# Seven weight buffers in place of four in the block-product stage, and token sums issued later in the program

## The chip, the cores and the metric

The kernel runs on one core of one Trainium2 chip. The metric is the device time of one execution in microseconds. A core has five engines with queues of their own, each strictly in order: TensorE (PE in the profile, PEld its weight loads) multiplies, VectorE (DVE) and ScalarE (ACT) work element by element, GpSimd (POOL) does small side work, and SyncE (SP) only issues DMA transfers. Engines wait for each other by semaphores. An instruction whose wait is not over holds back everything behind it in its queue.

## The reference

One layer of an encoder block on 512 tokens of width 1024, in float32: a half-step SwiGLU, a mixing sublayer with two attentions, a second half-step SwiGLU, and a last norm.

```python
h = modulate(rmsnorm(x, ffn1_norm), sh1, sc1)
x = x + 0.5 * g1 * swiglu(h, ffn1_w_in, ffn1_w_out)
h = modulate(rmsnorm(x, mix_norm), sh2, sc2)
...                                   # MLA and chunk attention on h @ w_in, gated and merged
x = x + g2 * (merged @ w_out)
h = modulate(rmsnorm(x, ffn2_norm), sh3, sc3)
x = x + 0.5 * g3 * swiglu(h, ffn2_w_in, ffn2_w_out)     # swiglu: silu(h@w_gate) * (h@w_up), then @ w_out
return rmsnorm(x, final_norm)
```

The change lies around the second SwiGLU: 1024 to 2 x 2816 columns (22 tiles of 128, gate and up), and back to 1024.

## The kernel before

Every float32 operand is cut into a rounded high part and the rest (`split`, L194 to L197: ScalarE casts the high part, VectorE subtracts it for the low part). A product is three matmuls: high by high, high by low, low by high (L212 to L214, and L584 to L586 in the block products). Weights come from HBM by SP into a ring of four buffers of 128x1024 (`raw`, L189 to L192); ScalarE writes `wh` from each and VectorE `wl`, in rings of three.

Around the change the stages follow each other so.

The mixing sublayer's output product (`down` with `w_out`) finishes one tile of 128 tokens after the other. Each is added to x, normed (`norm_token`, L231; the reciprocal root `rstd` is made by GpSimd, L219) and queued for `turn_token` (L244), in which TensorE transposes it, VectorE and ScalarE scale it (L255, L257), and the two split it into `h_hi` and `h_lo`. After tiles 1 and 3, `mix_tokens` (L269) makes sums and differences of the two tiles just done (L275 to L278, on VectorE) and splits four of these into `sum_h` and `sum_l`.

`up_plain` (L540) makes the first two of the 22 column tiles the plain way, in four jobs of 24 matmul pairs or triples each: jobs 0, 1 and 2 first for the first 256 tokens, then for the other 256, and job 3 for all 512 at once. Before jobs 0 and 2 it lets one pending token tile be turned, so that tiles 2 and 3 are transposed between the jobs.

`up_fast` (L570) makes the other 20 column tiles by a two-by-two block scheme with seven products in place of eight (order 1, 5, 6, 3, 7, 2, 4). For each it loads two weight buffers a and b, forms differences of their halves on VectorE (L599, L600, L603), splits a, the differences and b, and runs 84 matmuls of 256 columns. Products 5, 6, 3, 7 use plain tokens or the token sums. ScalarE copies partial results out (L611 to L618) and applies silu (L624, L625).

Then `down` with `w2b` (L637) brings the result back to 1024; its first loads, the gate vector for this sublayer (`ada_acc`, L284, with loads of `w_ada`) and the reload of x (`x_last`, L1068, issued by ScalarE) are mixed into the last block products.

The order on TensorE is that of the code. On VectorE, ScalarE, GpSimd and SP a scheduler sets it when the program is built: it takes work in the order of the code as buffers and data come free by its own estimate. So a line that is moved in the code, or a buffer more, moves other instructions too.

Three buffers matter beside the `raw` ring: two of 128x1024 with the tag `gate` (gate vectors, `vs` of the attention, the last norm's gain `final_gain`), and one with the tag `ada` (`o32` of the attention, then `ada_acc`).

Of the kernel before, what the change touches and what calls it, by code (L numbers as in the profile page):

```python
# [10 lines left out]
F32 = mybir.dt.float32  # L11
# [7 lines left out]
P = 128  # L19
S = 512  # L20
D = 1024
# [129 lines left out]
class Block:  # L151
# [91 lines left out]
    def turn_token(self, t, which, xn):  # L243
        nc = self.nc  # L244
        h32 = xn.rearrange("p (k c) -> p k c", k=KT)
        ts = slice(t * P, (t + 1) * P)
        for g in range(2):
            pt = self.bank("t")
            for j in range(4):
                nc.tensor.transpose(pt[:, j * P:(j + 1) * P], xn[:, (4 * g + j) * P:(4 * g + j + 1) * P], self.ident)  # L250
            for j in range(4):
                k = 4 * g + j
                sc, sh = self.scale[which][:, k:k + 1], self.shift[which][:, k:k + 1]
                if j < TURN_DVE:
                    nc.vector.tensor_scalar(h32[:, k], pt[:, j * P:(j + 1) * P], sc, sh, op0=ALU.mult, op1=ALU.add)  # L255
                else:
                    nc.scalar.activation(h32[:, k], pt[:, j * P:(j + 1) * P], AF.Identity, scale=sc, bias=sh)  # L257
            ks = slice(4 * g, 4 * g + 4)
            self.split(h32[:, ks], self.hH[:, ks, ts], self.hL[:, ks, ts])
        if which == 2:  # L260
            self.mixed.append(h32)
            if t % 2:
                self.mix_tokens(t // 2, *self.mixed[-2:])

    @staticmethod
    def halves(ap):
        return ap.rearrange("p k (a b c) -> p k a b c", a=2, b=2)

    def mix_tokens(self, j, ha, hb):  # L269
        nc = self.nc  # L270
        if not j:
            self.sums = [[self.slot([P, KT // 2, S // 2], F32R, "sum_" + p) for p in "hl"] for _ in range(4)]
        a11, a12, a21, a22 = (h[:, ks] for h in (ha, hb) for ks in (slice(0, 4), slice(4, 8)))
        tt = nc.vector.tensor_tensor
        tt(a22, a21, a22, op=ALU.add)  # L275
        tt(a21, a21, a11, op=ALU.subtract)
        tt(a11, a22, a11, op=ALU.subtract)
        tt(a12, a12, a11, op=ALU.subtract)  # L278
        cs = slice(j * P, (j + 1) * P)
        for (h, l), part in zip(self.sums, (a22, a11, a21, a12)):  # L280
            self.split(part, h[:, :, cs], l[:, :, cs])
# [254 lines left out]
    def up_plain(self, w1, fs, early, flush):  # L536
        nc = self.nc
        jobs = [(f, gu) for f in fs for gu in range(2)]
        ps, units, done = {}, {}, 0

        def mms(job, n0, n1):
            hi, lo = units[job]
            ns = slice(n0, n1)
            for k in range(KT):
                cs = slice(k * P, (k + 1) * P)
                self.mm3(ps[job][:, ns], (hi[:, cs], lo[:, cs]), (self.hH[:, k, ns], self.hL[:, k, ns]),
                         k == 0 and n0 == 0, k == KT - 1 and n1 == S)

        for i, job in enumerate(jobs):
            f, gu = job  # L550
            units[job] = self.unit(D, w1[f, gu])
            ps[job] = self.bank("o" if f % 2 and gu else "mm")
            if i < early:
                if i in flush:
                    self.flush()
                mms(job, 0, S // 2)
                if i < early - 1:
                    continue
                for late in jobs[:early]:
                    mms(late, S // 2, S)  # L560
            else:
                mms(job, 0, S)
            while done < len(fs) and (fs[done], 1) in ps:
                n = fs[done]
                sc = self.sc4((P, S))
                nc.scalar.activation(sc, ps[n, 0], AF.Silu)
                nc.vector.tensor_tensor(self.act_tile(n), sc, ps[n, 1], op=ALU.mult)
                done += 1

    def up_fast(self, w1, fs):  # L570
        nc = self.nc
        work = self.fix.tile([P, 2, 3, 512], F32, tag="x16", name="w_sums")
        hH, hL = (self.halves(z) for z in (self.hH, self.hL))
        plain = lambda k0, b: [[z[:, k0 + k, :, b] for z in (hH, hL)] for k in range(4)]
        mixed = lambda i: [[z[:, k] for z in self.sums[i]] for k in range(4)]
        lefts = {1: plain(0, 0), 2: plain(4, 0), 3: mixed(3), 4: plain(4, 1), 5: mixed(0), 6: mixed(1), 7: mixed(2)}
        left_half = slice(0, 256)

        def product(p, ps, w, start):
            hi, lo = w  # L580
            for k, (lh, ll) in enumerate(lefts[p]):
                cs = slice(k * P, (k + 1) * P)
                mm = nc.tensor.matmul
                mm(ps, hi[:, cs], lh, start=start and k == 0, stop=False, skip_group_check=not start)  # L584
                mm(ps, hi[:, cs], ll, start=False, stop=False, skip_group_check=not start)  # L585
                mm(ps, lo[:, cs], lh, start=False, stop=k == 3, skip_group_check=not start)  # L586

        def parts(src):
            hi = self.ring.tile([P, D], F32R, tag="wh", name="wh")
            lo = self.ring.tile([P, D], F32R, tag="wl", name="wl")  # L590
            self.split(src, hi, lo)
            return [(hi[:, cs], lo[:, cs]) for cs in (slice(0, 512), slice(512, 1024))]

        for n, f in enumerate(fs):
            a, b = (self.raw(D, w1[f, i]) for i in range(2))
            t = work[:, n % 2]
            tt = nc.vector.tensor_tensor
            b21, b12 = b[:, :512], b[:, 512:]
            tt(t[:, 0:2], b12.unsqueeze(1).to_broadcast([P, 2, 512]), a.rearrange("p (i c) -> p i c", i=2), op=ALU.subtract)  # L599
            tt(b12, a[:, 512:], t[:, 0], op=ALU.subtract)  # L600
            w11, w22 = parts(a)
            w1s, w3s = parts(t[:, 0:2].rearrange("p i c -> p (i c)"))
            tt(t[:, 2], b21, b12, op=ALU.subtract)  # L603
            w21, w2s = parts(b)
            last = self.slot([P, 2, 512], F32R, "w_last")
            self.split(t[:, 2], last[:, 0], last[:, 1])
            x, v = self.bank("s")[:, left_half], self.bank("t")[:, left_half]
            z, y = self.bank("mm")[:, left_half], self.bank("o")[:, left_half]
            s = self.sc4((P, 4, 256))
            product(1, x, w11, True)  # L610
            nc.scalar.copy(z, x)  # L611
            product(5, v, w1s, True)
            nc.scalar.copy(s[:, 1], v)
            product(6, x, w2s, False)
            nc.scalar.copy(s[:, 0], x)  # L615
            product(3, v, w22, False)
            product(7, x, w3s, False)
            nc.scalar.copy(y, x)  # L618
            tt(s[:, 2], v, s[:, 0], op=ALU.add)
            product(2, z, w21, False)  # L620
            tt(s[:, 3], x, s[:, 1], op=ALU.add)
            product(4, y, (last[:, 0], last[:, 1]), False)
            g = self.sc4((P, 2, 256))
            nc.scalar.activation(g[:, 0], z, AF.Silu)  # L624
            nc.scalar.activation(g[:, 1], y, AF.Silu)  # L625
            out = self.act_tile(f).rearrange("p (a b c) -> p b a c", a=2, b=2)
            four = lambda q: q.rearrange("p b (a c) -> p b a c", a=2)
            tt(out, four(s[:, 2:4]), four(g), op=ALU.mult)

    def act_parts(self, u):  # L630
        pair = [self.slot([P, 2, S], F32R, "act_" + p) for p in "hl"]
        self.split(self.acts[u], *pair)
        return [[z[:, j] for z in pair] for j in range(2)]

    def down(self, parts, nk, w2, layer, tail, after, lag=0, store=None, side=None):
        nc = self.nc
        nu = nk // 2  # L637
# [399 lines left out]
    def layer(self, banks):  # L1037
        nc, io = self.nc, self.io
# [7 lines left out]
        parts = lambda u: [[acts[2 * u + j][:, i] for i in range(2)] for j in range(2)]  # L1046
        self.down(parts, NF, io["w2a"], 0, 3, lambda t, xn: self.norm_token(t, 1, xn), LAG_DOWN)
        self.mix(lambda t, xn: self.norm_token(t, 2, xn))
        fin = self.fix.tile([P, D], F32, tag="gate", name="final_gain", bufs=2)
        nc.scalar.dma_start(fin, io["final"].to_broadcast([P, D]))  # L1050

        def finish(t, o32):
            z = self.slot([P, D], F32, "out")
# [9 lines left out]
            nc.scalar.dma_start(self.x_home[t], self.x[:, t])  # L1063
        self.up_plain(io["w1b"], range(F2), EARLY_UP, FLUSH_UP)
        self.up_fast(io["w1b"], range(F2, NF))
        self.x = self.fix.tile([P, NT, D], F32, tag="x16", name="x_last")
        for t in range(NT):
            nc.scalar.dma_start(self.x[:, t], self.x_home[t])  # L1068
# [85 lines left out]
```

## Time and profile before

| What | Value |
|---|---|
| Time, median of 3 runs | 1128.69 us (1128.15 to 1130.97) |
| The profiled execution | 1128.05 us, its span 1126.3 us |
| PE busy | 1091.5 us (97%), 5884 matmuls |
| DVE busy | 697.3 us (62%) |
| ACT busy | 525.1 us (47%) |
| POOL busy | 136.9 us (12%) |
| Mean granted TensorE clock | 0.997 of full speed |
| HBM | 142.55 MB read, 132 GB/s over the span |
| Weight load `raw<-w1b` | 512 KB, 3.5 us from issue to landing |

The time is told for the whole execution, the span for the part that the hardware profiler sees; 1.75 us lie around it. The stages named above lie at 756 to 785 us (`up_plain`), 785 to 992 us (`up_fast`) and from 992 us on (`down` with `w2b`). A busy share is an average over stages; where a stage loses time is seen from the stretches in which PE stands still and from what ended each.

### The profile page before, as it was taken

How to read it: one execution, taken by the hardware profiler on the slowest of the kernel's cores; microseconds unless marked ns; L12 is line 12 of the kernel's file. 1: busy time of each engine (PE TensorE's matmuls, PEld its weight loads, DVE VectorE, ACT ScalarE, POOL GpSimd, SP SyncE). 2: the span in 40 equal slices, each digit the busy share in tenths (PEclk: the TensorE clock that was granted, in tenths of full speed). 3: DMA queues.
4: the chain of work that ended last, by engine and by line, in shares of the span. 5: the costliest groups of instructions: out<-in, count | busy, mean ns of one | idle time of the engine just before them, and what ended most of it. 6: DMA issues, size and time to landing. Idle time of an engine off the chain costs nothing.

```text
span 1126.3 us, 15321 instructions
## 1 busy us (share of the span) xinstructions
PE 1091.5 (97%) x5884; PEld 928.9 (82%) x5884; DVE 697.3 (62%) x1170; ACT 525.1 (47%) x963; POOL 136.9 (12%) x126
## 2 busy tenths in 40 slices
PE   5999999999999999999999999999999999999997
PEld 4788888878888898988887888888999999978885
DVE  5886565663232676666677723568777777786724
ACT  5533222223121476666666633346555554654512
POOL 1000000000000012243344354100000000000100
PEclk9999999999999999999999999999999999999999
DMA  9677666663333620112223233522333333484312
GB/s 361 227 255 243 205 206 212 202 222 110 94 94 96 217 94 19 57 57 69 91 77 90 69 103 104 206 87 82 95 112 97 95 111 113 124 268 132 94 56 75
DMA packets 42992, 149.85 MB, mean 133 GB/s; under 512 B 5155, under 2 KB 5155, under 8 KB 42918
## 3 DMA queue, kind: packets, MB, share of 16 engines
q1 hardware_dynamic: 38160, 136.20, 37.6%
q10 hardware_dynamic: 4758, 12.66, 3.1%
q8 instruction: 46, 0.75, 0.3%
q14 instruction: 28, 0.23, 0.1%
HBM read 142.55 MB, written 6.29 MB: 132 GB/s over the span
## 4 chain that ended last, share of the span: by engine, by line
PE 76%; DVE 8%; DMA 8%; ACT 4%; issue 3%; POOL 0%; ACTq 0%; DVEq 0%; POOLq 0%
PE ps_mm L212 11%; PE ps_mm L214 11%; PE ps_mm L213 11%; DMA raw<-w_ada 6%; PE ps_s L213 3%; PE ps_s L214 3%; PE ps_s L212 3%; DVE wl L197 2%; PE ps_s L586 2%; PE ps_t L212 2%; PE ps_t L214 2%; PE ps_t L213 2%; PE ps_s L584 2%; PE ps_s L585 2%; PE ps_o L214 2%
## 5 line engine op out<-in xcount | busy, mean ns | idle before, releaser
L196 ACT CAST wh<-raw 128x1024 fp32r<-128x1024 f32 x170 | 178.1, 1051 | 244.9 <-PE ps_t L214 75.0
L197 DVE TENSOR_TENSOR wl<-raw,wh 128x1024 fp32r<-128x1024 f32 x138 | 168.5, 1224 | 116.8 <-ACT wh L196 116.4
L214 PE MATMUL ps_mm<-h_hi,wl 128*128 128x512 f32 (+1 forms) x464 | 178.9, 386 | 3.0 <-DVE wl L197 2.8
L212 PE MATMUL ps_mm<-h_hi,wh 128*128 128x512 f32 (+1 forms) x464 | 181.3, 391 | 0.0
L213 PE MATMUL ps_mm<-h_lo,wh 128*128 128x512 f32 (+1 forms) x464 | 178.5, 385 | 0.1
L214 PEld LDWEIGHTS ps_mm<-h_hi,wl 128*128 128x128 f32 x464 | 88.0, 190 | 22.6 <-DVE wl L197 3.8
L213 PEld LDWEIGHTS ps_mm<-h_lo,wh 128*128 128x128 f32 x464 | 88.1, 190 | 16.3 <-DVE h_lo L197 0.3
L212 PEld LDWEIGHTS ps_mm<-h_hi,wh 128*128 128x128 f32 x464 | 88.1, 190 | 15.9
L197 POOL TENSOR_TENSOR wl<-raw,wh 128x1024 fp32r<-128x1024 f32 x32 | 77.2, 2414 | 76.7 <-ACT wh L196 73.0
L288 DVE CUSTOM_DVE_ANT_0 raw<-raw,c_row,cols_sb 128x1024 f32<-128x1024 f32 x32 | 41.1, 1285 | 49.9 <-DMA raw<-w_ada 49.9
L219 POOL TENSOR_TENSOR rstd<-ss,neghalf 128x1 f32<-128x1 f32 x16 | 12.1, 758 | 409.9 <-DVE ss L229 400.4
L599 DVE TENSOR_TENSOR w_sums<-raw 128x1024 f32<-128x1024 f32 x20 | 24.5, 1225 | 46.0 <-DMA raw<-w1b 46.0
L196 ACT CAST act<-sc 128x512 fp32r<-128x512 f32 x22 | 13.6, 622 | 81.4 <-DVE sc L504 81.4
L83 ACT ACTIVATE sc<-sc,stat 128x128 f32<-128x128 f32 (+1 forms) x64 | 35.9, 562 | 29.5 <-DVE stat L81 29.3
L586 PE MATMUL ps_s<-sum_h,wl 128*128 128x256 f32 x160 | 44.8, 280 | 1.1 <-DVE wl L197 1.1
L586 PE MATMUL ps_t<-sum_h,wl 128*128 128x256 f32 x160 | 44.9, 281 | 0.4 <-DVE wl L197 0.4
L584 PE MATMUL ps_s<-sum_h,wh 128*128 128x256 f32 x160 | 44.8, 280 | 0.6 <-ACT sc L615 0.6
L584 PE MATMUL ps_t<-sum_h,wh 128*128 128x256 f32 x160 | 44.7, 279 | 0.0
L585 PE MATMUL ps_t<-sum_l,wh 128*128 128x256 f32 x160 | 44.7, 279 | 0.0
L585 PE MATMUL ps_s<-sum_l,wh 128*128 128x256 f32 x160 | 44.6, 279 | 0.0
L1054 POOL TENSOR_TENSOR out<-x_last,final_gain 128x512 f32<-128x512 f32 x4 | 7.2, 1810 | 301.6 <-DVE act_l L197 301.6
L284 DVE SCALAR_TENSOR_TENSOR ada_acc<-raw,cact,ada_acc 128x1024 f32<-128x1024 f32 x24 | 30.8, 1282 | 20.0 <-DMA raw<-w_ada 20.0
(390 smaller groups left out, 2879.0 us busy)
## 6 DMA issues: line engine op xcount, KB each, us to landing
raw<-w_ada SPq DMA_DIRECT2D x56, 512.0 KB, 4.5
raw<-w1b SPq DMA_DIRECT2D x44, 512.0 KB, 3.5
raw<-w1a SPq DMA_DIRECT2D x38, 512.0 KB, 3.9
raw<-w2a SPq DMA_DIRECT2D x22, 512.0 KB, 3.6
raw<-w2b SPq DMA_DIRECT2D x22, 512.0 KB, 4.1
w_first<-w_first SPq DMA_DIRECT2D x16, 512.0 KB, 9.3
raw<-w_gate SPq DMA_DIRECT2D x16, 512.0 KB, 3.7
raw<-w_ca SPq DMA_DIRECT2D x8, 512.0 KB, 4.4
```

Source lines behind the costliest of these rows:

```text
L83: nc.scalar.activation(p, p, AF.Exp, scale=-1.0, bias=low, accum_out=tot)
L196: nc.scalar.copy(hi, src)
L197: (low_engine or nc.vector).tensor_tensor(lo, src, hi.bitcast(F32), op=ALU.subtract)
L212: mm(ps, lh, rh, start=start, stop=False)
L213: mm(ps, lh, rl, start=False, stop=False)
L214: mm(ps, ll, rh, start=False, stop=stop)
L284: self.nc.vector.scalar_tensor_tensor(acc, w, self.cact[:, j:j + 1], acc, op0=ALU.mult, op1=ALU.add)
L288: self.nc.vector.tensor_tensor_reduce(w, w, self.c_row, 1.0, self.cols[:, b:b + 1], ALU.mult, ALU.add, out)
L584: mm(ps, hi[:, cs], lh, start=start and k == 0, stop=False, skip_group_check=not start)
L585: mm(ps, hi[:, cs], ll, start=False, stop=False, skip_group_check=not start)
L586: mm(ps, lo[:, cs], lh, start=False, stop=k == 3, skip_group_check=not start)
L599: tt(t[:, 0:2], b12.unsqueeze(1).to_broadcast([P, 2, 512]), a.rearrange("p (i c) -> p i c", i=2), op=ALU.subtract)
```

## The change

`mix_tokens` is no longer called by `turn_token`. `up_plain` calls it: for the tiles 0 and 1 once jobs 0 to 2 are recorded, for the tiles 2 and 3 after job 3. The sums are the same, in the same number.

In `up_fast` the weight loads go by turns through seven buffers: four of the `raw` ring, the two with the tag `gate` (named `raw_g`), and the one with the tag `ada` (`raw_a`). The load of `final_gain`, which held one of the two `gate` buffers from before the stage, comes after it. The buffer of `ada_acc`, which was cleared by GpSimd before the stage, is now free only after the last `raw_a`.

```diff
         if which == 2:
             self.mixed.append(h32)
-            if t % 2:
-                self.mix_tokens(t // 2, *self.mixed[-2:])
...
                 for late in jobs[:early]:
                     mms(late, S // 2, S)
+                self.mix_tokens(0)
             else:
                 mms(job, 0, S)
+                if i == early:
+                    self.mix_tokens(1)
...
+        def load(n, i, src):
+            m = (2 * n + i) % 7
+            if m < 4:
+                return self.raw(D, src)
+            if m < 6:
+                tile_ = self.fix.tile([P, D], F32, tag="gate", name="raw_g", bufs=2)
+            else:
+                tile_ = self.main.tile([P, D], F32, tag="ada", name="raw_a", bufs=1)
+            nc.sync.dma_start(tile_, src)
+            return tile_
+
         for n, f in enumerate(fs):
-            a, b = (self.raw(D, w1[f, i]) for i in range(2))
+            a, b = (load(n, i, w1[f, i]) for i in range(2))
...
-        fin = self.fix.tile([P, D], F32, tag="gate", name="final_gain", bufs=2)
-        nc.scalar.dma_start(fin, io["final"].to_broadcast([P, D]))
...
         self.up_fast(io["w1b"], range(F2, NF))
+        fin = self.fix.tile([P, D], F32, tag="gate", name="final_gain", bufs=2)
+        nc.scalar.dma_start(fin, io["final"].to_broadcast([P, D]))
```

TensorE's order is the same in both programs, matmul for matmul. The other queues move at three places.

**VectorE at the start of `up_plain`.** The names: `wl_6283` before and `wl_6261` now are the low part of job 1's weights, `wl_6314` and `wl_6292` that of job 2's; `xn_2` and `sum_l` belong to the token sums, `sc4_6139` is token tile 2, `sc4_6213` and `sc4_6193` tile 3. Before:

```order
L668 TENSOR_TENSOR x_back_5854<-x_back_5854,sc4_6213 128x512
L275 TENSOR_TENSOR xn_2_6091<-xn_2_6091 128x512
L255 TENSOR_SCALAR sc4_6139<-ps_t_6245,scale2_83,shift2_86 128x128
L276 TENSOR_TENSOR xn_2_6091<-xn_2_6091,xn_2_6058 128x512
L197 TENSOR_TENSOR sum_l_6170<-xn_2_6091,sum_h_6169 128x4x128
L277 TENSOR_TENSOR xn_2_6058<-xn_2_6091,xn_2_6058 128x512
L229 TENSOR_TENSOR ss_89<-ss_89 128x1
L197 TENSOR_TENSOR wl_6283<-raw_6280,wh_6282 128x1024
L278 TENSOR_TENSOR xn_2_6058<-xn_2_6058 128x512
L197 TENSOR_TENSOR sum_l_6172<-xn_2_6058,sum_h_6171 128x4x128
L236 TENSOR_SCALAR sc4_6213<-x_back_5854,rstd_90 128x1024
```

The same place now:

```order
L681 TENSOR_TENSOR x_back_5854<-x_back_5854,sc4_6193 128x512
L255 TENSOR_SCALAR sc4_6139<-ps_t_6223,scale2_83,shift2_86 128x128
L197 TENSOR_TENSOR wl_6261<-raw_6258,wh_6260 128x1024
L229 TENSOR_TENSOR ss_89<-ss_89 128x1
L274 TENSOR_TENSOR xn_2_6091<-xn_2_6091 128x512
L236 TENSOR_SCALAR sc4_6193<-x_back_5854,rstd_90 128x1024
L275 TENSOR_TENSOR xn_2_6091<-xn_2_6091,xn_2_6058 128x512
L276 TENSOR_TENSOR xn_2_6058<-xn_2_6091,xn_2_6058 128x512
L197 TENSOR_TENSOR h_lo_75<-sc4_6139,h_hi_74 128x4x128
L277 TENSOR_TENSOR xn_2_6058<-xn_2_6058 128x512
L255 TENSOR_SCALAR sc4_6193<-ps_t_6296,scale2_83,shift2_86 128x128
L197 TENSOR_TENSOR wl_6292<-raw_6289,wh_6291 128x1024
```

Job 1's `wl` has moved ahead of all token sums. The four sums of `mix_tokens` (L274 to L277) now stand between it and job 2's `wl`. Behind that `wl` come, in this order, `h_lo` of tile 2, the scaling of tile 3, one `sum_l`, `h_lo` of tile 3's first half, one weight difference (L612), one `sum_l`, and `h_lo` of tile 3's second half.

**VectorE within the block products.** One block of the middle of the stage, from the gated result of the block before (`act`) on; `raw_7340` and `raw_7338` before, `raw_7459` and `raw_7457` now are the two weight buffers of the next block. Before:

```order
L599 TENSOR_TENSOR w_sums_6486<-raw_7340,raw_7338 128x1024
L600 TENSOR_TENSOR raw_7340<-raw_7338,w_sums_6486 128x512
L619 TENSOR_TENSOR sc4_7121<-ps_t_7118,sc4_7121 128x256
L603 TENSOR_TENSOR w_sums_6486<-raw_7340 128x512
L197 TENSOR_TENSOR wl_7223<-raw_7216,wh_7222 128x1024
L621 TENSOR_TENSOR sc4_7121<-ps_s_7117,sc4_7121 128x256
L197 TENSOR_TENSOR wl_7227<-w_sums_6486,wh_7226 128x1024
L197 TENSOR_TENSOR wl_7232<-raw_7218,wh_7231 128x1024
L628 TENSOR_TENSOR act_7093<-sc4_7121,sc4_7212 128x2x2x128
```

Now:

```order
L612 TENSOR_TENSOR w_sums_6484<-raw_7459,raw_7457 128x1024
L613 TENSOR_TENSOR raw_7459<-raw_7457,w_sums_6484 128x512
L616 TENSOR_TENSOR w_sums_6484<-raw_7459 128x512
L632 TENSOR_TENSOR sc4_7240<-ps_t_7237,sc4_7240 128x256
L197 TENSOR_TENSOR wl_7343<-raw_7336,wh_7342 128x1024
L197 TENSOR_TENSOR wl_7347<-w_sums_6484,wh_7346 128x1024
L634 TENSOR_TENSOR sc4_7240<-ps_s_7236,sc4_7240 128x256
L197 TENSOR_TENSOR wl_7352<-raw_7338,wh_7351 128x1024
L641 TENSOR_TENSOR act_7334<-sc4_7240,sc4_7331 128x2x2x128
```

All three differences of a later block's weights now stand ahead of the first addition that waits for TensorE, so that nothing but that addition stands before the block's first `wl`.

**ScalarE at the end of the block products.** `wh_8928` is the high part of the first weights of `down`; `ps_mm` and `ps_o` at the silu lines (L624 and L625 before, L637 and L638 now) are the last block's two results. Before:

```order
L196 CAST act_h_8972<-act_6607 128x1024
L1068 DMA x_last_8917<-x_home0_70 128x1024
L615 COPY sc4_8822<-ps_s_8818 128x256
L1068 DMA x_last_8917<-x_home1_71 128x1024
L1068 DMA x_last_8917<-x_home2_72 128x1024
L618 COPY ps_o_8821<-ps_s_8818 128x256
L624 ACTIVATE sc4_8913<-ps_mm_8820 128x256
L1068 DMA x_last_8917<-x_home3_73 128x1024
L625 ACTIVATE sc4_8913<-ps_o_8821 128x256
L196 CAST wh_8928<-raw_8926 128x1024
```

Now:

```order
L1081 DMA x_last_8917<-x_home0_70 128x1024
L626 COPY sc4_8820<-ps_t_8817 128x256
L628 COPY sc4_8820<-ps_s_8816 128x256
L1081 DMA x_last_8917<-x_home1_71 128x1024
L1081 DMA x_last_8917<-x_home2_72 128x1024
L631 COPY ps_o_8819<-ps_s_8816 128x256
L1081 DMA x_last_8917<-x_home3_73 128x1024
L637 ACTIVATE sc4_8911<-ps_mm_8818 128x256
L196 CAST wh_8928<-raw_8926 128x1024
L638 ACTIVATE sc4_8911<-ps_o_8819 128x256
```

The cast of `wh_8928` has moved ahead of the last silu. The first issue of `x_last` has moved one copy earlier.

In SP's queue two loads of `w1b`, one into a `gate` buffer and one into the `ada` buffer, now stand far ahead of the stage: behind the loads of `w_gate` for the attention's end, and before the load of `w_br_b` that was next there, three more loads like it and the eight of `w_out`. GpSimd's clearing of `ada_acc` moves from there to the end of `up_fast`, and with it ScalarE's load of `b_ada` into it.

## Rows read from the trace of the kernel before

**Rows 1.** Waits of PE, 740 to 1127 us: total, times, longest.

```profile
PE ps_mm L214 <- DVE wl L197: 2.8, 2, 2.4
```

**Rows 2.** Stretches: busy by engine (all, then PE alone), PEclk, DMA share, GB/s.

```profile
762.00:765.00 3.00, 3.00 (x14) 3.00 (x15) 2.56 (x5) 3.00 (x8) 1.48 (x1) 0.50 0.53 175
...
992.00:994.00 2.00, 0.50 (x1) 1.00 1.00 270
```

**Rows 3.** Timeline of PE, 759 to 768 us: start, duration, instruction.

```profile
759.25 0.28 PE L213 MATMUL ps_mm<-h_lo,wh 128*128 128x256 f32 x1
761.92 0.58 PE L214 MATMUL ps_mm<-h_hi,wl 128*128 128x256 f32 x1 [2.40 <-DVE wl L197]
...
765.45 0.28 PE L212 MATMUL ps_mm<-h_hi,wh 128*128 128x256 f32 x1
...
766.02 0.28 PE L214 MATMUL ps_mm<-h_hi,wl 128*128 128x256 f32 x1
766.14 1.04 PE L250 MATMUL ps_t<-ident,sc 128*128 128x128 f32 x8
766.93 0.37 PE L212 MATMUL ps_mm<-h_hi,wh 128*128 128x256 f32 x1
...
767.86 0.38 PE L214 MATMUL ps_mm<-h_hi,wl 128*128 128x256 f32 x1 [0.45 <-DVE wl L197]
```

**Rows 4.** Timeline of DVE, ACT and POOL around the same place.

```profile
755.12 1.04 ACT L196 CAST wh<-raw 128x1024 fp32r<-128x1024 f32 x1
...
757.86 0.68 DVE L275 TENSOR_TENSOR xn<-xn 128x512 f32<-128x512 f32 x1
758.46 0.40 DVE L255 TENSOR_SCALAR sc<-ps_t,scale,shift 128x128 f32<-128x128 f32 x1
...
760.65 1.22 DVE L197 TENSOR_TENSOR wl<-raw,wh 128x1024 fp32r<-128x1024 f32 x1
...
763.51 0.75 DVE L236 TENSOR_SCALAR sc<-x_back,rstd 128x1024 f32<-128x1024 f32 x1 [0.44 <-POOL rstd L219]
```

**Rows 5.** Timeline of POOL: the roots of token tiles 2 and 3.

```profile
752.22 0.55 POOL L219 TENSOR_TENSOR rstd<-ss,neghalf 128x1 f32<-128x1 f32 x1 [6.05 <-DVE ss L229]
...
760.81 2.67 POOL L219 TENSOR_TENSOR rstd<-ss,neghalf 128x1 f32<-128x1 f32 x1 [8.05 <-DVE ss L229]
```

**Rows 6.** Timeline of PE: first matmul of four of the 20 blocks.

```profile
785.15 0.28 PE L584 MATMUL ps_s<-h_hi,wh 128*128 128x256 f32 x1
...
796.54 0.28 PE L584 MATMUL ps_s<-h_hi,wh 128*128 128x256 f32 x1
...
806.55 0.28 PE L584 MATMUL ps_s<-h_hi,wh 128*128 128x256 f32 x1
...
981.18 0.28 PE L584 MATMUL ps_s<-h_hi,wh 128*128 128x256 f32 x1
```

**Rows 7.** Waits of DVE, 785 to 988 us: total, times, longest.

```profile
DVE w_sums L599 <- DMA raw<-w1b: 46.0, 19, 4.6
```

**Rows 8.** Timeline of PE and ACT where the blocks end.

```profile
990.55 0.39 ACT L624 ACTIVATE sc<-ps_mm 128x256 f32<-128x256 f32 x1 [1.02 <-PE ps_mm L586]
...
991.67 0.28 PE L586 MATMUL ps_o<-h_hi,w_last 128*128 128x256 f32 x1
...
992.27 2.93 ACT L196 CAST wh<-raw 128x1024 fp32r<-128x1024 f32 x3
...
993.36 0.50 PE L212 MATMUL ps_s<-wh,act_h 128*128 128x512 f32 x1 [1.41 <-ACT wh L196]
994.62 0.50 PE L213 MATMUL ps_s<-wl,act_h 128*128 128x512 f32 x1 [0.76 <-DVE wl L197]
```

**Rows 9.** Timeline of DVE and SP at the attention's end.

```profile
652.66 0.69 DVE L197 TENSOR_TENSOR o_hl<-o,o_hl 128x512 fp32r<-128x512 f32 x1 [0.76 <-ACT o_hl L196]
...
656.83 0.33 SPq L191 DMA_DIRECT2D raw<-w_br_b  x1
680.97 4.19 SPq L191 DMA_DIRECT2D raw<-w_out  x2
```

More of the change, by code (lines that the diff above doesn't have):

```diff
@@ L267, in halves, with mix_tokens @@
         return ap.rearrange("p k (a b c) -> p k a b c", a=2, b=2)
-    def mix_tokens(self, j, ha, hb):
+    def mix_tokens(self, j):
         nc = self.nc
+        ha, hb = self.mixed[2 * j:2 * j + 2]
         if not j:
```

## The prediction, made before the changed kernel had run

> **What bounds the kernel now.** I read the page's engine totals first: PE is busy 97% of the span, so only the moments in which it stands still, or runs slowly, can be won. TensorE's order does not change, so the change acts through waits alone. The waits of PE from 740 us on come next [rows 1]: in `up_plain` it waited twice for VectorE's `wl`, 2.8 us, of which one wait was 2.4. The stretches then show the clock [rows 2]: after that wait TensorE had a granted clock of 0.50, its lower level of 1.2 GHz, from 762 to 765 us. From 992 to 994 us, with two waits close together, it kept 1.00. The timelines price the places [rows 3, 4, 6, 8]. Last, VectorE's waits within the blocks [rows 7]: in 19 of the 20 it stood before the weight difference L599 until the load landed, 46.0 us in all, up to 4.6. PE hardly shows those as waits of its own; they are seen in the distance from block to block.
>
> Each cost below is a loss of TensorE: the start of a matmul less the start it would have had one step after the one before it. A step of 256 columns at full clock is (766.02 - 765.45) / 5 = 0.114 us [rows 3].
>
> **Part 1: the start of `up_plain`.** What is lost there now. Job 1's first `wl` matmul started at 761.92; one step after 759.25 it would have started at 759.36. That is 2.56. The 16 matmuls from there to 765.45 took 3.53 where 16 steps take 1.82: 1.7 for the clock. Job 2's `wl` matmul stood at 767.86 where two steps after 766.93 are 767.16: 0.7. Sum 5.0.
>
> What will be lost. VectorE starts an instruction about 0.08 before the one ahead of it has ended (757.86 + 0.68 against 758.46, rows 4), so the steps are 0.60 for a 512-column instruction, 0.32 for L255, 1.14 for a `wl`, 0.67 for L236 [rows 4].
>
> Job 1: L255 takes the place of L275 at 757.86, `wl` starts at 758.18 and ends at 759.40. Its high part was cast by 755.12 + 1.04 = 756.16 [rows 4]. TensorE wants it at 759.36: lost 0.1.
>
> Job 2: token tile 3 has to be normed, turned and scaled. Its root on GpSimd can start about 759.7, behind `ss`. The same instruction took 0.55 for tile 2 and 2.67 for tile 3 [rows 5]. The long one ended 0.4 after a run of VectorE instructions had ended (L236 followed it after an idle 0.44, rows 4), so I take it to have been held up by them. Now one token sum lies beside it, and VectorE itself then waits: root at 760.65, L236 at 760.7. Three token sums, one `h_lo`, L255 and `wl` follow: 760.7 + 0.67 + 4 x 0.60 + 0.32 + 1.22 = 765.3. TensorE finishes job 1 at 759.45 + 22 x 0.114 = 761.95, turns tile 3 (766.93 - 766.02 - 0.114 = 0.8, rows 3), does two matmuls and wants `wl` at 763.0. Lost 2.3. So the wait has not gone; it has moved from job 1 to job 2, because the sums now stand ahead of job 2's `wl`.
>
> The Trainium skill's page "SBUF — State Buffer" (section "SBUF: two separate sides") bears on the root: a VectorE instruction with two SBUF inputs holds a pair of ports against a GpSimd instruction that reads SBUF, and the loser blocks fully. The pair 0.55 and 2.67 agrees. By that rule the sum stands as above; were the 2.67 the instruction's own cost, it would be the third rival's.
>
> Behind job 2: VectorE's next are `h_lo`, L255, a sum's low part, `h_lo`, a weight difference of 1.14, another low part, and the `h_lo` of tile 3's second half: 764.1 + 1.14 + 0.60 + 0.32 + 2 x 0.60 + 1.14 + 0.60 = 769.1, ending 769.8. TensorE wants it at 765.3 + 35 x 0.114 = 769.3: lost 0.5.
>
> The clock: a pause of 2.56 was followed by the lower level, one of 1.57 (below) was not [rows 2, 8]. 2.3 is nearer to the first, but its place against the earlier activity differs. If the clock falls it costs 1.7, less the 0.5 that is then covered: 1.2. I take half, 0.6. The sum now: 0.1 + 2.3 + 0.5 + 0.6 = 3.5, against 5.0. Part 1 gains 1.5. Bounds: 5.0 gained if no wait stays; 0.6 lost if the root takes its 2.67 and the clock falls (third rival).
>
> The Trainium skill's page "TensorE: Matmul & The Clock Gate" (section "HAM oscillation — how this bites in real kernels") says that a long enough idle stretch brings TensorE back to the lower rate, and that the work behind it then starts there. By that rule alone the term is 0 or 1.2, and this trace shows both outcomes.
>
> **Part 2: the blocks.** From the first block's start to the 20th's are 981.18 - 785.15 = 196.03 us for 19 blocks. The second took 806.55 - 796.54 = 10.01, the first 796.54 - 785.15 = 11.39, the other 17 on average (981.18 - 806.55) / 17 = 10.27 [rows 6]. Each block has the same instructions on every engine. The reason that the order and rows 7 give: L599 waits for a load, and block n+1's first `wl` stands behind it, so that product 1 gets its `wl` late. With four buffers a load can go out only when the block before has split its weights. With seven it goes out some three blocks ahead; 3.5 us from issue to landing are then far under the cover of 30. Then VectorE's work of one block (three `wl` and L599 at 1.14, five of 512 columns at 0.60, two of 256 at some 0.3) is about 8.2 us of 10.0, and it is done before TensorE asks. So all blocks go to 10.01: 19 x 10.01 = 190.2, gained 5.8. I take 5.6, since ScalarE's copy before product 4 may still slip. The first block's excess is VectorE's too (a `wl` behind L599 and a gated result); there the loads of the new program are in by then. Bounds: 0, if the loads are not what delays `wl`; 5.8, if all blocks reach the second's length.
>
> **Part 3: the end of the blocks.** The 20th block ran from 981.18 to 991.67 + 0.11 = 991.79, 10.6 [rows 6, 8]: 0.6 lost, where the copy L615 stood behind the issue of `x_last`. The issue now comes a copy earlier, but waits for a VectorE instruction that is no longer behind an `ada_acc` step; yet two such steps, each waiting for a load of `w_ada`, now stand before the last block's first `wl`. I keep 0.3 of the 0.6 as gained. Then `down`: its first matmul at 993.36 is 1.57 late, its second at 994.62 another 1.0 (a step of 512 columns is twice 0.114). Now the cast of `wh_8928` follows the first silu, not the second: 990.55 + 0.38 = 990.9, done 991.95; the first matmul is 0.2 late. The `wl`, 1.22 long, is done at 993.2 against 992.25: 1.0 late as before. Gained 1.4. Part 3 gains 1.7; bounds 1.8 lost (a load of `w_ada` late by all of the 3.5 that a load takes) and 3.2 gained.
>
> **What costs nothing.** The clearing of `ada_acc` and the load of `b_ada` leave a place where PE does not wait, and come to one where GpSimd is idle. The load of `final_gain` has the whole of `down` before it is read. The two early loads in SP's queue wait for buffers that come free at 653.4, when `o_hl` is split, and the next load went out only at 656.83 [rows 9]; cover 3.4 us.
>
> **Sum.** 1.5 + 5.6 + 1.7 = 8.8. Against the profiled execution, 1128.05 (span 1126.3 and 1.75 around it): 1119.2. The median of the runs shown is 0.6 above that execution; I keep 1119.2 and let the range carry the rest.
>
> **The rivals.**
> 1. The clock does not fall, all blocks reach 10.01 and part 3 goes fully: 2.1 + 5.8 + 3.2 = 11.1, so 1117.0. For it: the pauses of 1.57 and 1.0, close together, left the clock at 1.00 [rows 2, 8]. Against: 2.3 is nearer to the 2.56 that did not, and the `wl` of `down` cannot come earlier than its cast.
> 2. The blocks stay as they are, since `wl` is late from its place behind ScalarE's cast and not from the load: part 2 gains only the first block's 1.4, and the time is 1128.05 - 1.5 - 1.4 - 1.7 = 1123.5. Against it: the short blocks had the same casts.
> 3. The root of tile 3 takes 2.67: `wl` of job 2 comes 1.7 later and the clock falls: part 1 loses 0.6, 1128.05 + 0.6 - 5.6 - 1.7 = 1121.3.
> 4. The change does not do what it says for the time: waits go elsewhere for as much as they give, 1127 to 1129.
> 5. Slower. SP's queue at the attention's end: the load into the `ada` buffer waits, and behind it stand the loads of `w_br_b`, `w_gate` and `w_out`. It decides from 656.83 on. Were the buffer held until the first `w_out` load's place (680.97, rows 9), the loads behind would be 24.1 late; two units already split, 24 matmuls of 2 x 0.114 each, cover 11, and TensorE would stand 13: 1119.2 + 13 = 1132. For it: one queue, strictly in order. Against: the buffer's last reader ends at 653.4.
>
> **How the numbers follow.** The forecast (1117.6 to 1120.4, with the clock's 1.2 either way) 0.50, rival 1 0.14, rival 2 0.10, rival 3 0.14, rival 4 0.07, rival 5 0.05. The range, 1115.5 to 1123.5, holds the forecast and rivals 1 and 3, and most of 2; about 2 in 10 stay outside. About 0.3%, 3.4 us, is what a measurement of this kernel can tell from no change. Faster by more (under 1125.3): the forecast, rivals 1 to 3, 0.88, less a little for their tails, 0.87. Within: 0.08. Slower: 0.05.
>
> **What would show it.** In the profile after: PE's wait for job 1's `wl` under 0.3, one for job 2's of about 2.3, and a stretch behind it with a clock of 0.50 or 1.00; tile 3's root of about 1 us; the 19 block distances within 0.1 of 10.0 and no wait of VectorE for `raw` there; the first matmul of `down` within 0.5 of the last block. The forecast is wrong if the blocks keep 10.2 with loads landed long before, or if PE waits anew before 756 us.

## The result and the profile after

The changed kernel took 1115.91 us (median of 5 runs, 1114.91 to 1117.85) against 1128.15 (5 runs, 1127.21 to 1130.97): a ratio of 0.9891, with a 95% interval of 0.9873 to 0.9908. That is 12.2 us less; 8.8 were forecast. The profiled execution took 1115.35 us with a span of 1113.6, against 1128.05 and 1126.3.

I read it in the same order as before. First the waits of PE from 740 us on, where [rows 1] stood (total in us, times, longest):

```profile
PE ps_mm L214 <- DVE wl L197: 2.0, 1, 2.0
PE ps_s L213 <- DVE wl L197: 0.8, 1, 0.8
PE ps_mm L213 <- DVE h_lo L197: 0.2, 1, 0.2
```

Three waits are left: job 2's `wl`, one `h_lo` behind it, and the second matmul of `down`. The stretch behind job 2's `wl`, which answers to [rows 2] (busy time of PE, PEld, DVE, ACT, POOL with their counts, then PEclk, DMA share, GB/s):

```profile
762.00:765.00 3.00, 1.04 (x9) 0.83 (x8) 3.00 (x6) 1.79 (x5) 0.00 (x0) 1.00 0.03 11
```

TensorE stood still for 2 of the 3 us, and its granted clock stayed at 1.00. Before, the same stretch ran at 0.50, the lower of its two levels. PE's timeline there, for [rows 3]:

```profile
758.50 0.38 PE L214 MATMUL ps_mm<-h_hi,wl 128*128 128x256 f32 x1
...
762.12 0.28 PE L213 MATMUL ps_mm<-h_lo,wh 128*128 128x256 f32 x1
764.36 0.39 PE L214 MATMUL ps_mm<-h_hi,wl 128*128 128x256 f32 x1 [1.96 <-DVE wl L197]
...
768.33 0.28 PE L212 MATMUL ps_mm<-h_hi,wh 128*128 128x256 f32 x1
768.83 0.39 PE L213 MATMUL ps_mm<-h_lo,wh 128*128 128x256 f32 x1 [0.22 <-DVE h_lo L197]
```

A job has 24 matmuls for each half of the tokens, in triples that need `wh`, `h_lo` and `wl`. Job 1's `wl` is 0.08 late (the matmul ahead of it started at 758.31, a step is 0.114), job 2's is 2.24 - 0.11 = 2.13 late, the `h_lo` 0.50 - 0.11 = 0.39. VectorE and GpSimd at the same place, for [rows 4, 5]:

```profile
757.24 1.21 DVE L197 TENSOR_TENSOR wl<-raw,wh 128x1024 fp32r<-128x1024 f32 x1
758.37 0.15 DVE L229 TENSOR_TENSOR ss<-ss 128x1 f32<-128x1 f32 x1
758.44 0.69 DVE L274 TENSOR_TENSOR xn<-xn 128x512 f32<-128x512 f32 x1
759.57 0.75 DVE L236 TENSOR_SCALAR sc<-x_back,rstd 128x1024 f32<-128x1024 f32 x1 [0.44 <-POOL rstd L219]
760.23 0.69 DVE L275 TENSOR_TENSOR xn<-xn,xn 128x512 f32<-128x512 f32 x1
760.95 0.69 DVE L276 TENSOR_TENSOR xn<-xn,xn 128x512 f32<-128x512 f32 x1
761.56 0.69 DVE L197 TENSOR_TENSOR h_lo<-sc,h_hi 128x512 fp32r<-128x512 f32 x1
762.16 0.69 DVE L277 TENSOR_TENSOR xn<-xn 128x512 f32<-128x512 f32 x1
762.77 0.41 DVE L255 TENSOR_SCALAR sc<-ps_t,scale,shift 128x128 f32<-128x128 f32 x1
763.09 1.22 DVE L197 TENSOR_TENSOR wl<-raw,wh 128x1024 fp32r<-128x1024 f32 x1
```

```profile
758.60 0.93 POOL L219 TENSOR_TENSOR rstd<-ss,neghalf 128x1 f32<-128x1 f32 x1 [6.77 <-DVE ss L229]
```

Job 1's `wl` now goes first; L275, L276, an `h_lo`, L277 and a scaling stand between tile 3's L236 and job 2's `wl`, as the prediction had it. The root of tile 3 took 0.93 in place of 2.67.

The blocks, for [rows 6, 7]: PE's first matmul of blocks 1, 2 and 20, and then VectorE's waits from 785 to 988 us.

```profile
781.23 0.28 PE L586 MATMUL ps_s<-h_hi,wh 128*128 128x256 f32 x1
...
791.24 0.28 PE L586 MATMUL ps_s<-h_hi,wh 128*128 128x256 f32 x1
...
970.59 0.28 PE L586 MATMUL ps_s<-h_hi,wh 128*128 128x256 f32 x1
```

```profile
DVE sc L632 <- PE ps_t L588: 23.6, 18, 2.8
DVE wl L197 <- ACT wh L196: 13.3, 37, 1.9
DVE ada_acc L283 <- DMA raw<-w_ada: 2.0, 3, 0.9
```

The 46.0 us of waits for the weights' loads are gone, and VectorE now waits for TensorE. The 19 distances are 9.94 to 10.01 and sum up to 189.36 (before 196.03). The end of the blocks, for [rows 8]:

```profile
980.69 0.50 PE L212 MATMUL ps_s<-wh,act_h 128*128 128x512 f32 x1
981.95 0.50 PE L213 MATMUL ps_s<-wl,act_h 128*128 128x512 f32 x1 [0.76 <-DVE wl L197]
982.28 0.40 PE L214 MATMUL ps_s<-wh,act_l 128*128 128x512 f32 x1
```

The first matmul of `down` comes 10.10 after the 20th block's start (before 12.18), the second is still 1.26 behind the first. Last, SP's queue at the attention's end, for [rows 9]:

```profile
652.43 0.33 SPq L604 DMA_DIRECT2D raw_a<-w1b  x1
655.90 0.33 SPq L191 DMA_DIRECT2D raw<-w_br_b  x1
```

The load that follows `raw_a` goes out 0.9 earlier than before (656.83), and the stage on TensorE starts 0.94 earlier (below), so nothing was held up.

From the first matmul of job 0 (755.38; before 756.32) to the third of `down` the time became 2.98 + 6.67 + 2.09 = 11.74 us shorter (the head of `up_plain`, the 19 block distances, the end). What is left of the 12.7 between the two profiles, 0.94, lies ahead of the stage, where TensorE does the same: in the 11 profiles of this study the stage began between 754.4 and 757.1 us.

### The profile page after: what moved, and what is told of

Its sections match the earlier page's. It is cut to its first block, busy times and chain, and to the rows that moved or that the text cites. A ratio compares the mean times of both kernels' runs of the same rounds, so it can differ in the third digit from the quotient of the medians.

```text
span 1113.6 us, 15325 instructions
## 1 busy us (share of the span) xinstructions
PE 1084.4 (97%) x5884; PEld 925.4 (83%) x5884; DVE 700.7 (63%) x1170; ACT 525.1 (47%) x963; POOL 134.7 (12%) x126
## 4 chain that ended last, share of the span: by engine, by line
PE 90%; DVE 4%; ACT 3%; DMA 1%; issue 1%; ACTq 0%; POOLq 0%
PE ps_mm L212 14%; PE ps_mm L213 14%; PE ps_mm L214 14%; PE ps_s L213 3%; PE ps_s L214 3%; PE ps_s L212 3%; PE ps_o L214 3%; PE ps_o L212 3%; PE ps_o L213 3%; PE ps_s L586 3%; PE ps_s L587 3%; PE ps_s L588 3%; PE ps_t L212 2%; PE ps_t L214 2%; PE ps_t L213 2%; PE ps_t L586 2%
## 5 line engine op out<-in xcount | busy, mean ns | idle before, releaser
L196 ACT CAST wh<-raw 128x1024 fp32r<-128x1024 f32 x154 | 161.7, 1051 | 255.7 <-PE ps_t L214 73.5
L197 DVE TENSOR_TENSOR wl<-raw,wh 128x1024 fp32r<-128x1024 f32 x122 | 149.3, 1225 | 125.4 <-ACT wh L196 124.9
L97 DVE TENSOR_TENSOR pt<-ps_t,pt 128x512 fp32r<-128x512 f32 (+1 forms) x64 | 30.9, 488 | 16.5 <-ACT pt L96 15.6
L197 DVE TENSOR_TENSOR act_l<-act,act_h 128x1024 fp32r<-128x1024 f32 x22 | 27.9, 1273 | 17.0 <-PE ps_t L213 15.9
```

The costliest lines, as they stand in the source:

```text
L97: nc.vector.tensor_tensor(pl[:, :n], pt[:, :n], ph[:, :n].bitcast(F32), op=ALU.subtract)
L196: nc.scalar.copy(hi, src)
L197: (low_engine or nc.vector).tensor_tensor(lo, src, hi.bitcast(F32), op=ALU.subtract)
```

## The experiments

Theory: three gains that don't depend on each other. The sums' new place shortens the head (from job 0's first matmul to the first block), the buffers shorten the blocks and their end. Rivals: all of it comes from the loads; or the sums' backlog on VectorE had kept the blocks slow. The stretches of each kernel's profiled execution, in us ("end" is from block 20's start to the third matmul of `down`; the clock is TensorE's granted level behind the head's longest pause; the last two columns are the median of the runs and its ratio to the kernel before on the same chip, whose median was 1127.80 beside e1 to e4, 1127.39 beside "after again" and e5 to e7, and 1128.19 beside e8):

| kernel | head | block 1 | blocks 2-19 | end | clock | median | ratio (95%) |
|---|---|---|---|---|---|---|---|
| before | 28.83 | 11.39 | 184.64 | 13.78 | 0.50 | 1128.15 | 1 |
| after | 25.85 | 10.01 | 179.35 | 11.69 | 1.00 | 1115.91 | 0.9891 (0.9873-0.9908) |
| after again | 26.10 | 10.05 | 179.99 | 11.56 | 1.00 | 1116.76 | 0.9903 (0.9887-0.9918) |
| e1 sums only | 25.84 | 10.01 | 183.96 | 13.73 | 1.00 | 1123.18 | 0.9959 (0.9946-0.9972) |
| e8 e1 + late load | 26.97 | 9.99 | 184.56 | 14.15 | 0.50 | 1124.60 | 0.9965 (0.9954-0.9976) |
| e2 buffers only | 28.83 | 10.95 | 179.25 | 11.52 | 1.00 | 1120.76 | 0.9932 (0.9920-0.9944) |
| e3 five buffers | 26.10 | 10.03 | 179.28 | 11.52 | 1.00 | 1116.85 | 0.9903 (0.9890-0.9916) |
| e4 wl first | 24.01 | 12.42 | 180.04 | 11.56 | 1.00 | 1117.24 | 0.9910 (0.9897-0.9923) |
| e5 copy first | 26.96 | 9.79 | 176.28 | 12.07 | 0.50 | 1113.16 | 0.9874 (0.9857-0.9890) |
| e6 sums behind wl | 24.63 | 9.99 | 179.30 | 11.75 | 1.00 | 1113.89 | 0.9884 (0.9865-0.9903) |
| e7 e5 and e6 | 24.65 | 9.80 | 176.27 | 11.65 | 1.00 | 1112.00 | 0.9861 (0.9844-0.9879) |

**e1: the sums alone.** The kernel before with `mix_tokens(0)` and `(1)` called in `up_plain` as in the change; nothing else.

```
             for late in jobs[:early]:
                 mms(late, S // 2, S)
+            self.mix_tokens(0)
         else:
             mms(job, 0, S)
+            if i == early:
+                self.mix_tokens(1)
```

> The kernel before with the token sums alone put later (four weight buffers, final_gain's load at its old place). Theory T (three separate gains: the sums' place gives the 3.0 us of the head of up_plain, the buffers give the 6.7 of the blocks and the 2.1 of their end): the head, from job 0's first matmul to the first block, takes 25.85 us as in the changed kernel and not 28.83; the clock behind job 2's pause of about 2 us stays at 1.00; the blocks stay as before (first distance 11.4, the later ones 10.27 on average); time about 1125.1 (before 1128.1). Rival A (the loads made the head slow too): no gain, 1128. Rival B (the sums' backlog on VectorE kept the blocks slow): the blocks fall to 10.0 here as well, 1119.

The head fell to 25.84, as the theory has it, and the end stayed. But 4.6 us were won by the medians (1127.80 - 1123.18) and not 3.0: block 1 fell to 10.01 as well. The sums, which stood ahead of its weights in VectorE's queue, account for its whole excess of 1.4 here, with no buffer added. Rival A falls, and rival B holds for that one block only: VectorE still waited for loads in the others, as this row of its waits from 785 to 985 us shows.

```profile
DVE w_sums L601 <- DMA raw<-w1b: 41.8, 17, 4.6
```

One more thing shows in this profile. At the start of `down` TensorE had the same two waits as in the kernel before [rows 8], where the clock stayed at 1.00 [rows 2]. Here it was 0.50 from 988.7 to 992.1, with steps of 0.42 where the kernel before has 0.23:

```profile
988.33 0.53 PE L213 MATMUL ps_s<-wl,act_h 128*128 128x512 f32 x1 [0.77 <-DVE wl L197]
988.66 0.62 PE L214 MATMUL ps_s<-wh,act_l 128*128 128x512 f32 x1
989.08 0.63 PE L212 MATMUL ps_s<-wh,act_h 128*128 128x512 f32 x1
```

**e2: the buffers alone.** The changed kernel with the sums back in `turn_token`.

```
         if which == 2:
             self.mixed.append(h32)
+            if t % 2:
+                self.mix_tokens(t // 2)
```

> The changed kernel with the token sums back at their old place (seven weight buffers, final_gain's load late). Theory T: head as before, 28.8 us with the 2.4 us wait for job 1's wl; the 19 block distances 9.94 to 10.01; the end as in the changed kernel; 1128.1 - 6.7 - 2.1 = 1119.3. Rival B (the sums' backlog kept the blocks slow): over 1122. Of the clock: if the pause of 2.4 us lowers it by its length or place, the stretch behind it shows 0.50 again as in the kernel before; if that was chance, it may show 1.00, and the head is then about 1.2 shorter.

Blocks 2 to 19 and the end are those of the changed kernel, the head is that of the kernel before. Block 1 takes 10.95: with the sums in their old place the buffers take 0.44 off it, so it is the one stretch in which the two parts of the change meet. By the medians 7.0 us are won (1127.80 - 1120.76); with e1's 4.6 that is 11.7, against 12.2 for the whole change on its own chip. The clock gave the surprise. PE's waits from 740 to 785 us, and the stretch behind the pause of 2.4:

```profile
PE ps_mm L214 <- DVE wl L197: 4.0, 2, 2.4
```

```profile
762.00:765.00 3.00, 2.25 (x19) 2.25 (x20) 2.56 (x4) 3.00 (x9) 2.31 (x1) 1.00 0.34 83
```

The same pause as before, and the clock did not fall. Yet the head is the same, 28.83: job 1 ran faster, and job 2 then waited for its `wl` 1.6 us (4.0 - 2.4) where it had waited 0.45 [rows 3]. VectorE ran the same list in both: counted from job 0's first matmul, each of its instructions up to the first block's last weight split (25.73 us behind it) starts within 0.02 us of the same time. TensorE came to their results earlier or later. So the fall of the clock had cost the kernel before nothing.

**e3: five buffers.**

```
-            m = (2 * n + i) % 7
+            m = (2 * n + i) % 5
```

(four `raw` and the one `ada` buffer).

> The changed kernel with five weight buffers in place of seven (four raw and the one that ada_acc's stage leaves). Theory T (only how early a load can go out matters): each load goes out about half a block, 5 us, earlier than with four; the longest wait before L599 was 4.6, so no wait is left, the distances are 9.94 to 10.01 and the time is that of the changed kernel, 1115.9. Rival (the last two buffers carry part of the gain): about a third to a half of the 6.7 us is lost again, 1118 to 1119, with waits of VectorE for raw left in the blocks.

As the theory has it: 179.28 for blocks 2 to 19, and 1.7 us of waits for loads are left of 46.0:

```profile
DVE w_sums L609 <- DMA raw<-w1b: 1.3, 4, 0.5
DVE w_sums L609 <- DMA raw_a<-w1b: 0.4, 2, 0.2
```

One buffer more than four does it; the sixth and seventh give nothing that can be seen here. Not shown apart from the loads is VectorE's order: with more buffers the scheduler also puts the weight differences earlier (section on the change), and no run kept that order with four.

**e4: job 2's `wl` first.** Tile 3's turning is queued behind job 2's `wl` (and, by the same line, tile 2's behind job 0's); the sums and the first block's weight difference behind tile 3's last `h_lo` (`last_wl` and `last_lo` are the VectorE instructions of those splits).

```
+                    with self.tc.issue_after(self.last_wl.ins):
+                        self.flush()
...
+                with self.tc.issue_after(self.last_lo.ins):
+                    self.mix_tokens(0)
...
+            with self.tc.issue_after(self.last_lo.ins):
+                tt(t[:, 0:2], b12..., op=ALU.subtract)
+                tt(b12, a[:, 512:], t[:, 0], op=ALU.subtract)
```

> The changed kernel with three groups of VectorE instructions queued behind others: tile 3's turning behind job 2's wl, and the token sums and the first block's weight difference behind tile 3's last h_lo. Theory T (job 2's wl is late only because sums stand ahead of it): wl ends at about 762.0 in place of 764.3, TensorE's waits for wl and h_lo fall from 2.13 and 0.39 us to under 0.3 together; the sums end later, and product 5 of the first block loses up to 0.5; time 1113.5 (1113.0 to 1114.2). Rival (VectorE's whole work between tile 3's root and the first block is the bound): what the head gives comes back as waits in job 3 and the first block, 1115.9 as the changed kernel.

The expectation failed and its rival held, with 1117.24 for its 1115.9. Job 2's wait went and the head fell by 1.84, but block 1 grew by 2.41. PE's waits from 755 to 795 us, and VectorE's from 757 to 791:

```profile
PE ps_s L590 <- DVE wl L197: 0.8, 1, 0.8
PE ps_t L590 <- DVE wl L197: 0.7, 1, 0.7
PE ps_mm L213 <- DVE h_lo L197: 0.3, 1, 0.3
```

```profile
DVE h_lo L197 <- ACT h_hi L196: 2.4, 2, 1.8
DVE sc L236 <- POOL rstd L219: 0.7, 1, 0.7
```

VectorE stood still for 2.4 us in front of `h_lo`, with the sums shut out behind it, and just that much was missing in block 1.

**The changed kernel again**, as the base of the next three.

> The changed kernel once more, as the base of the next three runs. 1115.9 again (1114.9 to 1117.9 was its spread); head 25.9, first block 10.0, blocks 9.94 to 9.99, last block to down's third matmul 11.5 to 11.7; the clock behind job 2's pause of 2 us at 1.00, as in the three profiles with that pause so far.

The same program gave distances of 10.00 in place of 9.97 on average: 0.7 us over the 19 that differ from one execution to the next. The head differed by 0.25.

**e5: the copy ahead of the cast.** In each block ScalarE's copy into `ps_o` is put ahead of the cast of the next block's `w_sums`.

```
-            w1s, w3s = parts(t[:, 0:2].rearrange("p i c -> p (i c)"))
+            with self.tc.issue_after(cp.ins) if n else nullcontext():
+                w1s, w3s = parts(t[:, 0:2].rearrange("p i c -> p (i c)"))
...
-            nc.scalar.copy(y, x)
+            cp = nc.scalar.copy(y, x)
```

> The changed kernel with one order of ScalarE fixed: in each block its copy of ps_s into ps_o (the start of product 4) comes ahead of the cast of the next block's w_sums, not behind it. Theory T (that copy is the only thing that keeps a block over its 84 steps and some): the two long steps at the start of product 4, 0.20 and 0.22, become 0.114 each, the distances 9.75 to 9.80, and 20 blocks give 3.8: 1112.1. Rival (the cast is what is needed next: moved behind the copy, its wl comes late for product 5): the blocks stay at 9.94 or more, 1115.9 or slower.

All 19 distances are 9.79 or 9.80, and 3.6 us are won (1116.76 - 1113.16). In the changed kernel the copy stood behind a cast of 1.05 us, and product 4 waited for it. ScalarE there, and PE:

```profile
868.08 1.05 ACT L196 CAST wh<-w_sums 128x1024 fp32r<-128x1024 f32 x1 [0.35 <-PE ps_s L587]
869.03 0.37 ACT L631 COPY ps_o<-ps_s 128x256 f32<-128x256 f32 x1
```

```profile
869.26 0.28 PE L588 MATMUL ps_mm<-h_hi,wl 128*128 128x256 f32 x1
869.46 0.39 PE L586 MATMUL ps_o<-h_hi,w_last 128*128 128x256 f32 x1
869.68 0.28 PE L587 MATMUL ps_o<-h_lo,w_last 128*128 128x256 f32 x1
```

Steps of 0.20 and 0.22, in every block, where the others of a block are 0.117 (the 0.114 of the expectation was the step of `up_plain`). That is 0.19 a block, and e5 gives back 0.18. What is left is the steps alone: in e5 one block's first matmul and the next one's, 84 matmuls later, lie 9.80 apart, and 84 x 0.117 is 9.8.

```profile
861.91 0.28 PE L586 MATMUL ps_s<-h_hi,wh 128*128 128x256 f32 x1
...
871.71 0.28 PE L586 MATMUL ps_s<-h_hi,wh 128*128 128x256 f32 x1
```

In this profile the clock fell behind job 2's pause of 1.96, and the head is 0.9 longer than that of the base.

**e6: the sums behind job 2's `wl` only.** As e4, with one condition changed (`wl2` is job 2's `wl`).

```
-                with self.tc.issue_after(self.last_lo.ins):
+                with self.tc.issue_after(wl2.ins):
                     self.mix_tokens(0)
```

> As e4, but the token sums are queued behind job 2's wl only, so that they fill the 2.4 us for which VectorE stood idle there. Theory T (VectorE's work up to the first block is the bound, so what counts is that it never idles): TensorE loses some 0.4 more at an h_lo than in e4, the head is 24.4, and the first block falls from 12.4 to about 10.4, together 34.8 against 35.9 in the changed kernel; 1114.8. Rival (the first block of e4 is late for another reason than VectorE's backlog): the first block stays near 12.4, 1117.

VectorE's wait for `h_hi` is gone, and its only idle time from 757 to 791 us is the root's:

```profile
DVE sc L236 <- POOL rstd L219: 0.7, 1, 0.7
```

Head and block 1 take 34.62 us against 36.15 in the base and 36.43 in e4; 34.8 was expected. The median is 2.9 below that of the base. The theory holds: up to the first block VectorE's work is the bound, and an order helps by what idle time of VectorE it fills.

**e7: e5 and e6 together.**

> e5 and e6 in one kernel. If both hold and don't touch each other, 3.8 + 1.1 off the changed kernel: 1111.0. If the first block's VectorE backlog delays the casts behind the copy, between 1112 and 1114.

From job 0 to `down` the profiles have 222.37 us against 227.70 in the base, 5.3 less. The parts are 1.5 (head and block 1 in e6) and 3.7 (blocks 2 to 19 in e5), so they add up. By the medians it is 4.8 less (1116.76 - 1112.00), close to the 4.9 expected, though e5 and e6 alone won 3.6 and 2.9 by theirs: with four runs each, the medians are not sharp enough for such a sum. This version has the lowest median; its interval overlaps that of e5.

**e8: four buffers with the late load of `final_gain`.** The changed kernel with `load()` taken out:

```
-            a, b = (load(n, i, w1[f, i]) for i in range(2))
+            a, b = (self.raw(D, w1[f, i]) for i in range(2))
```

> The changed kernel with four weight buffers again: the sums' place and the late load of final_gain stay. Against e1 it differs by that load's place alone. Theory T (the 2.1 us at the end of the blocks come from the buffers, since ScalarE's cast of down's first weights stands behind both silus here, as before): head 25.8 to 26.1, first distance 10.0, the others 10.2 on average, from the last block to down's third matmul 13.7; 1123, as e1. Rival (the end comes from the load's new place): the last stretch is 11.5 to 11.7 and the time 1121.

The end is 14.15 (13.73 in e1), so its 2.1 us come from the buffers and not from that load's place. Of the 0.4 over e1, 0.25 is the step to the third matmul of `down`, 0.59 in place of 0.34: as in e1 the clock fell to 0.50 there, at 989.2, here ahead of that step. The opposite, seven buffers with the load early, was not tried: `final_gain` would then hold one of the two `gate` buffers that the weights use. The clock fell behind job 2's pause too, and the head is 26.97:

```profile
764.00:767.00 3.00, 3.00 (x16) 3.00 (x15) 3.00 (x5) 3.00 (x8) 0.00 (x0) 0.50 0.55 175
```

## Why the prediction was right, and where its sizes were off

The direction and the mechanism of each part held, and each of the three sizes was too small. The sum was 8.8; measured were 11.7 within the stage and 12.2 by the medians. So 1115.91 lies under the forecast's own 1117.6 to 1120.4, and only 0.4 inside the range. That the range held it is in part luck: what came is nearest to rival 1, which had a chance of 0.14.

**Part 1 (1.5 forecast, 2.98 in the profile).** The three terms of what is lost now held. The late `wl` moved from job 1 to job 2 as worked out: 0.08, 2.13 and 0.39 lost, where 0.1, 2.3 and 0.5 were expected. The mis-sized term is the clock. Half of 1.2 was put in; in this execution it was 0. Half was a fair price: of the six profiles with this pause of 1.9 to 2.0 us the clock fell in two, e5 and e8. There the head took 26.96 and 26.97, against 25.84 to 26.10 in the other four, so the price is 0.9 to 1.1, near the 1.2. The Trainium skill's page "TensorE: Matmul & The Clock Gate" (section "HAM oscillation — how this bites in real kernels") says that a long enough idle stretch brings the lower rate. Behind this pause the runs show both outcomes, with the same order of work on TensorE up to there; no one kernel was profiled with both. The clock's 0.6 leaves 0.9 of the 1.48. Of this 0.3 are the smaller waits (2.6 in place of 2.9), and 0.6 are losses before that were not counted: with 2.6 lost now and 2.98 won, 5.6 were lost before, and not 5.0. One is the `h_lo` at the start of job 0's second half (a step of 0.41 in place of 0.114 there), and behind job 2's `wl` the steps were 0.118, where they are 0.114 in the profile after.

The working also listed the clock's 1.7 as a loss of the kernel before. e2 shows that it was none by itself: at full clock job 2's step grew from 0.73 to 1.86, and smaller waits beside it made up the rest. In the third rival the terms add up to a loss of 0.8 (0.1 + 4.0 + 1.7 - 5.0), not 0.6; its time moves by 0.2.

The root of tile 3 was read rightly, as held up by VectorE, and rival 3 fell. It took 2.67 with a `wl` and two sum instructions beside it (before, e2), 0.93 with one (after), and 0.55 in e4, e6 and e7, where VectorE stood idle. The Trainium skill's page "SBUF — State Buffer" (section "SBUF: two separate sides") says that a VectorE instruction with two SBUF inputs and a GpSimd instruction that reads SBUF lock each other out; the three durations agree.

**Part 2 (5.6 forecast, 6.67).** The term that was mis-sized is "all blocks go to 10.01". The distances became 9.94 to 10.01, 9.97 on average: 19 x 0.044 = 0.83 more; the 0.2 kept back for product 4's copy make the rest. But "after again" has 10.00 with the same program, where 0.15 is left of the 0.83; so most of it is no more than the executions differ. Nor was 10.01 the floor for which it was taken: the second block of the kernel before had product 4's late copy in it, with steps of 0.25 and 0.22 there. Counting shows it: 84 steps of 0.117, the step within the blocks, are 9.8, and the 0.2 over that has a reason. e5 found it and won all of it. One cause was named in part: the first block's 1.4 was put down to VectorE's queue and to loads. e1 and e8 give all of it back with four buffers, by the sums' place; the buffers by themselves give 0.44 (e2). Rival 2 fell: e1 and e8 keep the loads' waits and the 10.2, e2 and e3 lose nearly all of the waits and the 10.2.

**Part 3 (1.7 forecast, 2.09).** All of it is the first matmul of `down` (12.18 to 10.10 after the block's start). Of block 20's 0.6 half was kept back and all came. That varies: in e5 PE waited 0.3 for L627's copy in the last block, and the end took 12.07. The second matmul is as late as it was, as forecast.

**The rivals.** The outcome lies past rival 1 (1117.0), whose three conditions all came close to true: no fall of the clock, blocks at 10.0 or under, 2.09 of 3.2 at the end. Rival 4 is outside the interval of the ratio, and rival 5 did not come: the loads behind `raw_a` went out earlier than before.

## What to carry to other kernels

Where a wait is for an engine that is never idle, an order of its queue moves the wait and does not remove it (e4); look for the moments in which that engine itself waits, and put the movable work there (e6). Before the best repetition of a loop is taken for its floor, count its steps, with the step as it is within that loop: what is over has a cause of its own (e5). A weight buffer pays as long as the loads still end waits: here one more than four was enough (e3).

## What the runs showed of the hardware

TensorE's clock after a pause of one length, at one place in the same order of work on TensorE, came out either way: after 1.9 to 2.0 us it stayed at 1.00 in four profiles and fell to 0.50 in two, and after 2.4 us it fell in the kernel before and stayed in e2. Behind the two waits of 1.4 and 0.8 us at the start of `down` it stayed in the kernel before and fell in e1 and e8. That it is chance, and not something in which these kernels differ, is likely but not shown, since no one kernel was profiled with both outcomes. For it speaks that the mean granted clock differs between runs of one kernel (0.994 to 0.999 in e8); a fall of 3.4 us makes 0.0015 of that, by estimate (half of 3.4 out of 1122). What a fall costs depends on what comes next: nothing where the next wait was for VectorE anyway (28.83 with and without it), about 1.0 us where it was not.
